# Gated linear attention on one core: two heads' outputs together, woven with the start of the output projection

## Chip, core and metric

The kernel runs on one core of a Trainium2 chip. The metric is the device time of one execution in microseconds (us), taken as the median of several runs. Lower is better.

## What is computed

The reference is a two-layer trunk over 512 positions of width 1024 in float32. The first layer mixes with a gMLP and latent attention, the second with gated linear attention; each mixer is followed by a layer norm, a squared-ReLU feed-forward network and another layer norm. The change lies in the second layer's mixer. Cut to that:

```python
def gla(q, k, v, log_a):                  # 4 heads, DK = 128, DV = 256, in chunks
    def step(state, xs):
        qi, ki, vi, gi = xs
        b = jnp.cumsum(gi, axis=2)
        o_inter = jnp.einsum('bhld,bhde->bhle', qi * jnp.exp(b), state)
        ...
        o = o_inter + jnp.einsum('bhts,bhse->bhte', attn, vi)
        b_last = b[:, :, -1:, :]
        state = (jnp.exp(b_last[:, :, 0, :])[..., None] * state
                 + jnp.einsum('bhsd,bhse->bhde', ki * jnp.exp(b_last - b), vi))
        return state, o
...
o = gla(q, k, v, log_a)
o = layer_norm(o, c_ln_g[j], c_ln_b[j]).astype(x.dtype).reshape(bn, s, hv)
y = (o * jax.nn.silu(g)) @ w_out_odd[j]
x = layer_norm(ALPHA * x + y, ln1_g[layer], ln1_b[layer])
```

## The kernel before

The kernel keeps the 512 positions as four blocks (chunks) of 128. A float32 product with a weight is made as three products of rounded halves (`mm3`, lines 159 to 161: high by high, high by low, low by high), 128x512 each, on TensorE. The halves are made by `split`: ScalarE casts the high half, VectorE subtracts to get the low half (lines 164 and 165). Weights come through three `raw` buffers by DMAs on SP's queue.

PSUM is given out in eight banks under four tags (`BANKS`, line 122): "mm" 3, "sc" 2, "o" 1, "tp" 2. A tile of a tag takes the banks of that tag in turn, so it waits until the last reader of the tile before it in that bank is done.

In `odd_mixer` each head goes through `chunk_steps` (line 1090), which makes the attention matrix `at`, the decayed query `qb`, the decayed and transposed key `kh` (transposed on TensorE, line 1161, copied by ScalarE, line 1163) and the decays `ebl`. Then `head_out` (line 1166) makes the outputs of a head, chunk by chunk: `su` = kh by V (line 1179), from which VectorE makes the next state (line 1182 for the first, line 1184 for the others), and `o1` = at by V plus qb by state (lines 1185 and 1187). Two chunks share one accumulator bank of 128x512. Each half is read by VectorE for its mean and variance (lines 1189 and 1190). After two chunks follow a reciprocal root in twelve small 128x2 steps on VectorE (`rsqrt_`, lines 173 to 182) and a thirteenth (line 1194), the normalisation of both halves on ScalarE (line 1197), and three 128x512 operations on VectorE (lines 1199, 1200, 1203), the last of which multiplies it into the gate tile `G`. `head_out` is a generator that yields after every chunk with an estimate of TensorE's time.

The heads' outputs are spread over the other work. `weave(a, b, n)` takes one step of b, then n steps of a, and so on. Head 0 is woven with the projection of head 3's query and key, head 1 with the second half of the gate's projection, head 2 with whatever is left of that (line 1266), and head 3 with `early` of `out_proj_odd` (line 1300). `early` transposes G of heads 0 and 1 (`y_T`, eight transposes a call over two banks of "tp" when two blocks are taken; line 194, then `split` into XH and XL) and runs the four first of eight row blocks of the output projection for (block, half) (0, 0), (1, 0) and (0, 1) (`part`, line 1280). Behind it stand the transposes of heads 2 and 3 and the other half of the sums, with a residual add (line 208) and its statistics (line 211).

TensorE's order is that of the program (`manual_schedule`). VectorE's order in this stage is a scheduler's, and from `in_order` (line 1305) on that of the program; ScalarE's is the scheduler's too. Each engine runs its own instructions strictly in that order.

Of the kernel before, what the change touches and what calls it, by code (L numbers as in the profile page):

```python
# [37 lines left out]
C_HEADS, C_DK, C_DV = 4, 128, 256  # L38
# [65 lines left out]
def trunk(ctx: ExitStack, tc: tile.TileContext, a: dict, out: bass.AP):  # L104
# [20 lines left out]
    def bank(name, tag=None):  # L125
        tag = tag or next(cycle)
        return ps.tile([P, 512], F32, tag=tag, name=name, bufs=BANKS[tag])
# [14 lines left out]
    def weave(a, b, n):  # L142

        live = True
        while live:
            live = False
            for g, m in ((b, 1), (a, n)):
                for _ in range(m):
                    c = next(g, None)
                    if c is None:  # L150
                        break
                    live = True
                    yield c

    def granules(w, r0, rows, kb, cols, pool=wp):
        return [granule(w[r:r + kb * P, cols], kb, cols.stop - cols.start, pool) for r in range(r0, r0 + rows, kb * P)]
# [10 lines left out]
    def rsqrt_(var, n, eps=LN_EPS):  # L167

        v = sm.tile([P, n], F32, tag=f"nv{n}", name="nv")
        w = sm.tile([P, n], F32, tag=f"nw{n}", name="nw")  # L170
        y = sm.tile([P, n], F32, tag=f"ny{n}", name="ny")
        t = sm.tile([P, n], F32, tag=f"nt{n}", name="nt")
        nc.vector.tensor_scalar(v, var, eps, None, ALU.add)
        nc.vector.tensor_scalar(w, var, eps, -0.5, ALU.add, ALU.mult)
        nc.vector.tensor_scalar(y.bitcast(I32), v.bitcast(I32), -0.5, MAGIC_RSQRT, ALU.mult, ALU.add)
        for _ in range(3):
            if n == 1:
                nc.vector.tensor_scalar(t, y, y, w, ALU.mult, ALU.mult)
            else:
                nc.vector.tensor_tensor(t, y, y, ALU.mult)  # L180
                nc.vector.tensor_tensor(t, t, w, ALU.mult)
            nc.vector.scalar_tensor_tensor(y, t, 1.5, y, ALU.add, ALU.mult)
        return y

    def tb(t):
        return slice(t * P, (t + 1) * P)

    def to_xT(src, k0, nk, t):

        for k in range(0, nk, 4):  # L190
            m = min(4, nk - k)
            pt = bank("xt", "tp")
            for j in range(m):
                nc.tensor.transpose(pt[:, j * P:(j + 1) * P], src[:, (k + j) * P:(k + j + 1) * P], ident)
            split(XH[:, k0 + k:k0 + k + m, tb(t)], XL[:, k0 + k:k0 + k + m, tb(t)],
                  pt[:, :m * P].rearrange("p (k c) -> p k c", k=m))

    def load_ln(g, b):
        nc.sync.dma_start(LG, g.partition_broadcast(P))
        nc.sync.dma_start(LB, b.partition_broadcast(P))  # L200

    def new_stats():
        return [sm.tile([P, 2, 6], F32, tag="st", name="st", bufs=8) for _ in range(NT)]
# [56 lines left out]
    def act_stat(acc, lh, ll, g, per, ks, last):  # L260

        for k in ks:
            wh, wl = g[k // per]
            mm3(acc, lh[k], ll[k], wh[:, k % per], wl[:, k % per], k == 0, k == last)

    def in_order():

        return tc.manual_schedule(engines={mybir.EngineType.DVE})

    def xblk(t):  # L270
        return [XH[:, k, tb(t)] for k in range(KD)], [XL[:, k, tb(t)] for k in range(KD)]
# [721 lines left out]
    def out_steps(gs, stats, accs):  # L993

        def mm(t, n, k0, k1):
            if (t, n) not in accs:
                accs[t, n] = bank("op"), 0
            acc, done = accs[t, n]
            act_stat(acc, *xblk(t), gs[n], 2, range(max(k0, done), k1), KD - 1)
            if k1 == KD:  # L1000
                add_half(t, n, acc, True, stats)
        return norms(mm, stats, lambda t: ff_T["now"](t))
# [13 lines left out]
    def odd_mixer(mp, v0_granules):  # L1016
# [3 lines left out]
        G = mp.tile([P, NT, HV], F32, name="G1")  # L1020
# [142 lines left out]
            nc.scalar.copy(kh[:, :NT - 1].rearrange("p c d -> p (c d)"), pt[:, :(NT - 1) * P])  # L1163
            heads[h] = (at, qb, kh, ebl)

        def head_out(h, tag="mm"):
            at, qb, kh, ebl = heads[h]
            hv = slice(h * C_DV, (h + 1) * C_DV)
            st = None
            for c2 in range(0, NT, 2):  # L1170
                op = bank("o1", tag).rearrange("p (c d) -> p c d", c=2)
                bst = sm.tile([P, 2, 6], F32, tag="bs", name="bs")
                mv = sm.tile([P, 2, 2], F32, tag="mv2", name="mv2")
                for c in (c2, c2 + 1):
                    o = op[:, c - c2]
                    sn = None
                    if c < NT - 1:
                        u = bank("su", "o")[:, :C_DV]
                        nc.tensor.matmul(u, kh[:, c], V[:, c, hv], start=True, stop=True)
                        sn = mp.tile([P, C_DV], F32, tag="state", name="state", bufs=3)  # L1180
                        if c == 0:
                            nc.vector.tensor_copy(sn, u)
                        else:
                            nc.vector.scalar_tensor_tensor(sn, st, ebl[:, c:c + 1], u, ALU.mult, ALU.add)
                    nc.tensor.matmul(o, at[:, c], V[:, c, hv], start=True, stop=c == 0)
                    if c > 0:
                        nc.tensor.matmul(o, qb[:, tb(c)], st, start=False, stop=True)
                    st = sn
                    nc.vector.bn_stats(bst[:, c - c2], o)
                    nc.vector.bn_aggr(mv[:, c - c2], bst[:, c - c2])  # L1190
                    yield 1.28 if 0 < c < NT - 1 else 0.85
                rs = rsqrt_(mv[:, :, 1], 2)
                nm = sm.tile([P, 2], F32, tag="nm", name="nm")
                nc.vector.scalar_tensor_tensor(nm, mv[:, :, 0], -1.0, rs, ALU.mult, ALU.mult)
                z = mp.tile([P, 2, C_DV], F32, tag="z", name="z", bufs=ZB)
                for i in range(2):
                    nc.scalar.activation(z[:, i], op[:, i], AF.Identity, scale=rs[:, i:i + 1], bias=nm[:, i:i + 1])
                bc = lambda w: w.unsqueeze(1).broadcast_to([P, 2, C_DV])
                nc.vector.tensor_tensor(z, z, bc(CG), ALU.mult)
                nc.vector.tensor_tensor(z, z, bc(CB), ALU.add)  # L1200
                while (True, c2 + 1, h // 2) not in done:
                    yield 0.0
                nc.vector.tensor_tensor(G[:, c2:c2 + 2, hv], G[:, c2:c2 + 2, hv], z, ALU.mult)
# [49 lines left out]
        fill.add(qk[2], 10.2)  # L1253
        fill.add(nat(G, 2 * HK + HV, 0, True), 20.5)
        ho0 = fill.add(weave(qk[3], head_out(0), 4), 14.5)
        g1w = weave(g1, head_out(1), 4)
        fill.add(g1w, 24.8)
        fill.run(2.5)
        for h in range(C_HEADS):
# [3 lines left out]
                fill.until(ho0, 1.8)  # L1263
            for _ in chunk_steps(h):
                fill.run(SLOT)
        for _ in weave(g1w, head_out(2), 3):
            pass
        return head_out, G

    def out_proj_odd(left):  # L1270
        head_out, G = left
        w = a["w_out_odd"][0]
        gs = [granules(w, 0, D, 2, slice(n * 512, (n + 1) * 512)) for n in range(2)]
        stats = new_stats()
        accs = {}

        def y_T(t, h0, nh):
            to_xT(G[:, t, h0 * C_DV:(h0 + nh) * C_DV], 2 * h0, 2 * nh, t)

        def part(t, n):  # L1280
            acc = bank("op", "mm")
            for k in range(4):
                act_stat(acc, *xblk(t), gs[n], 2, [k], KD - 1)
                yield 0.64
            accs[t, n] = acc, 4

        def early():
            y_T(0, 0, 2)
            yield 0.43
            y_T(1, 0, 2)  # L1290
            yield 0.43
            yield from part(0, 0)
            y_T(2, 0, 2)
            yield 0.43
            y_T(3, 0, 2)
            yield 0.43
            yield from part(1, 0)
            yield from part(0, 1)

        for _ in weave(early(), head_out(3, "sc"), 2):  # L1300
            pass
        load_ln(a["ln1_g"][1], a["ln1_b"][1])

        steps = out_steps(gs, stats, accs)
        with in_order():
            y_T(0, 2, 2)
            y_T(1, 2, 2)
            next(steps)
            y_T(2, 2, 2)
            y_T(3, 2, 2)  # L1310
        return steps
# [3 lines left out]
    with tc.tile_pool(name="m0", bufs=1) as mp:  # L1315
        left = even_mixer(mp)
# [5 lines left out]
    with tc.tile_pool(name="m1", bufs=1) as mp:  # L1322
        steps = out_proj_odd(odd_mixer(mp, v0))
# [41 lines left out]
```

## Time and profile before

| what | us |
|---|---|
| median of three runs | 1166.93 |
| lowest and highest of them | 1166.70 and 1167.01 |
| the profiled execution, its own time | 1167.06 |
| its span, from first to last instruction | 1165.4 |
| TensorE busy in the span | 1140.8 |
| VectorE busy | 827.6 |
| ScalarE busy | 517.0 |

The span is what the trace shows; the execution's own time is 1.66 us longer than it. A busy TensorE includes pipelined tails: the ends of matmuls are modelled, and one row's busy time lies partly under the next one's. Idle time of an engine is shown in the timeline in square brackets with what ended it.

### The profile page before, as it was taken

Reading aid. Unit: us, or ns where it says so; the run is one execution under the profiler, and the core shown is the slowest. Engines: PE = TensorE matmul, PEld = TensorE weight load, DVE = VectorE, ACT = ScalarE, POOL = GpSimd, SP = SyncE. Lnnn points to the kernel's source line nnn. Section 1 sums busy time; section 2 is a strip of 40 time slices with the busy share of each in tenths; the row PEclk is TensorE's granted clock in tenths of the full one; section 3 lists DMA queues with packets and bytes.
Section 4 is the critical chain, followed back from the end, with each engine's and each line's share of the span. In section 5 each row is a group of like instructions: output and inputs, shape, how many; then the busy total and the mean of one; then the engine's idle time right before and its main releaser. Section 6 shows DMA issues by size and latency. Waiting matters only on the chain.

```text
span 1165.4 us, 17129 instructions
## 1 busy us (share of the span) xinstructions
PE 1140.8 (98%) x6884; PEld 994.6 (85%) x6884; DVE 827.6 (71%) x1562; ACT 517.0 (44%) x801; POOL 4.5 (0%) x13
## 2 busy tenths in 40 slices
PE   8999999999999999999999999999999999999997
PEld 7988788898889998997888888778997899889986
DVE  6745687786766867658758559898767577676665
ACT  6367462444343634543264433442534436345330
POOL 0000000000000000000000000000000000000000
PEclk9999999999999999999999999999999999999999
DMA  8413143133312342224325312211133224314121
GB/s 269 125 37 109 55 130 107 37 109 109 127 62 84 128 127 84 79 79 135 75 95 145 91 55 73 73 66 62 62 125 116 90 80 142 129 38 127 55 91 55
DMA packets 84207, 111.68 MB, mean 96 GB/s; under 512 B 6080, under 2 KB 53056, under 8 KB 84128
## 3 DMA queue, kind: packets, MB, share of 16 engines
q1 hardware_dynamic: 84128, 110.59, 30.0%
q8 instruction: 54, 0.88, 0.3%
q14 instruction: 25, 0.20, 0.1%
HBM read 108.47 MB, written 2.10 MB: 95 GB/s over the span
## 4 chain that ended last, share of the span: by engine, by line
PE 89%; DVE 6%; ACT 4%; DMA 0%; issue 0%; SPq 0%; DVEq 0%; ACTq 0%
PE f L451 23%; PE f L161 10%; PE f L160 10%; PE f L159 10%; PE vg L159 3%; PE vg L160 3%; PE vg L161 3%; PE op L159 3%; PE op L161 3%; PE op L160 2%; PE sc L843 1%; PE qk L159 1%; PE qk L160 1%; PE qk L161 1%; PE o L865 1%; PE pl L1129 1%
## 5 line engine op out<-in xcount | busy, mean ns | idle before, releaser
L161 PE MATMUL f<-whi,hl 128*128 128x512 f32 x448 | 177.4, 396 | 5.5 <-DVE hl L431 5.5
L159 PE MATMUL f<-whi,hh 128*128 128x512 f32 x448 | 177.2, 396 | 1.0 <-ACT hh L430 1.0
L164 ACT CAST whi<-cr 128x1024 fp32r<-128x1024 f32 x98 | 100.8, 1048 | 174.0 <-PE f L161 81.1
L160 PE MATMUL f<-wlo,hh 128*128 128x512 f32 x448 | 176.8, 395 | 0.0
L164 ACT CAST whi<-raw 128x1024 fp32r<-128x1024 f32 (+3 forms) x117 | 118.4, 1019 | 99.1 <-PE f L451 35.7
L165 DVE TENSOR_TENSOR wlo<-raw,whi 128x1024 fp32r<-128x1024 f32 (+3 forms) x117 | 138.0, 1186 | 26.5 <-ACT whi L164 26.5
L165 DVE TENSOR_TENSOR wlo<-cr,whi 128x1024 fp32r<-128x1024 f32 x98 | 119.3, 1221 | 23.0 <-ACT whi L164 23.0
L451 PE MATMUL f<-XH,wlo 128*128 128x256 f32 x448 | 125.9, 281 | 0.0
L451 PE MATMUL f<-XH,whi 128*128 128x256 f32 x448 | 125.8, 281 | 0.0
L451 PE MATMUL f<-XL,whi 128*128 128x256 f32 x448 | 125.8, 281 | 0.0
L161 PEld LDWEIGHTS f<-whi,hl 128*128 128x128 f32 x448 | 84.3, 188 | 27.7 <-DVE hl L431 8.1
L208 DVE SCALAR_TENSOR_TENSOR XN<-XN,f 128x512 f32<-128x512 f32 (+1 forms) x113 | 74.4, 679 | 42.6 <-PE f L161 42.1
L159 PEld LDWEIGHTS f<-whi,hh 128*128 128x128 f32 x448 | 84.3, 188 | 20.8 <-ACT hh L430 1.8
L160 PEld LDWEIGHTS f<-wlo,hh 128*128 128x128 f32 x448 | 84.3, 188 | 19.3
L451 PE MATMUL f<-sl,whi 128*128 128x256 f32 x336 | 94.6, 281 | 0.0
L451 PE MATMUL f<-sh,wlo 128*128 128x256 f32 x336 | 94.5, 281 | 0.0
L451 PE MATMUL f<-sh,whi 128*128 128x256 f32 x336 | 94.5, 281 | 0.0
L431 DVE TENSOR_TENSOR hl<-r,hh 128x512 fp32r<-128x512 f32 x64 | 44.2, 690 | 60.6 <-ACT hh L430 60.6
L451 PEld LDWEIGHTS f<-XL,whi 128*128 128x128 f32 x448 | 84.4, 188 | 0.5
L451 PEld LDWEIGHTS f<-XH,whi 128*128 128x128 f32 x448 | 84.4, 188 | 0.5
L451 PEld LDWEIGHTS f<-XH,wlo 128*128 128x128 f32 x448 | 84.4, 188 | 0.0
L451 PEld LDWEIGHTS f<-sh,whi 128*128 128x128 f32 x336 | 63.3, 188 | 0.0
(268 smaller groups left out, 2396.8 us busy)
## 6 DMA issues: line engine op xcount, KB each, us to landing
raw<-in_w_ff SPq DMA_DIRECT2D x70, 512.0 KB, 4.1
cr<-in_w_ff SPq DMA_DIRECT2D x58, 512.0 KB, 4.0
raw<-in_w_in_odd SPq DMA_DIRECT2D x24, 512.0 KB, 4.2
XN<-in_x SPq DMA_DIRECT2D x16, 256.0 KB, 3.4
raw<-in_w_in_even SPq DMA_DIRECT2D x8, 512.0 KB, 4.6
raw<-in_w_out_even SPq DMA_DIRECT2D x8, 512.0 KB, 3.8
raw<-in_w_out_odd SPq DMA_DIRECT2D x8, 512.0 KB, 3.6
LB<-in_ln_b SPq DMA_DIRECT2D x4, 512.0 KB, 3.8
```

The source lines that it names most:

```text
L159: nc.tensor.matmul(acc, lh, rh, start=first, stop=False)
L160: nc.tensor.matmul(acc, lh, rl, start=False, stop=False)
L161: nc.tensor.matmul(acc, ll, rh, start=False, stop=last)
L164: nc.scalar.copy(hi, src)
L165: nc.vector.tensor_tensor(lo, src, hi.bitcast(F32), ALU.subtract)
L208: nc.vector.scalar_tensor_tensor(x, x, ALPHA if first else 1.0, acc, ALU.mult, ALU.add)
L431: late.append(lambda: nc.vector.tensor_tensor(f(hl), r, f(hh).bitcast(F32), ALU.subtract))
L451: nc.tensor.matmul(d, l, r, start=first and j == k == i == 0, stop=j == 1 and k == HK_ - 1 and i == 2, skip_group_check=True)
L843: nc.tensor.matmul(sc[:, :N], qts[t][:B_QK, h, :], KT[:, h, :N], start=True, stop=True)
L865: nc.tensor.matmul(os[t][:, h, :], pT[:, j * P:(j + 1) * P], V[:, j, h, :], start=j == 0, stop=j == t)
L1129: nc.tensor.matmul(pl[:, c * 64:(c + 1) * 64], x[:, tb(c)], x[:, tb(c)].rearrange("p (n two k) -> p n two k", two=2, k=H)[:, :, 1], start= ...
```

## The change

Head 2's outputs no longer run by themselves behind what is left of the gate's projection. Heads 2 and 3 are woven with each other, one chunk of head 3, then one of head 2, and that sequence is woven with `early`, two steps of `early` for each chunk. Both heads' accumulators come from the two "sc" banks (head 2 had "mm" before). Head 3's `su` comes from the "tp" banks, which the transposes use as well; head 2's `su` stays in the single "o" bank. The number of instructions is the same on every engine.

```diff
-        def head_out(h, tag="mm"):
+        def head_out(h, tag="mm", state_tag="o"):
             at, qb, kh, ebl = heads[h]
...
                     if c < NT - 1:
-                        u = bank("su", "o")[:, :C_DV]
+                        u = bank("su", state_tag)[:, :C_DV]
...
-        for _ in weave(g1w, head_out(2), 3):
+        for _ in g1w:
             pass
-        return head_out, G
+        return weave(head_out(2, "sc"), head_out(3, "sc", "tp"), 1), G
 
     def out_proj_odd(left):
-        head_out, G = left
+        last_heads, G = left
...
-        for _ in weave(early(), head_out(3, "sc"), 2):
+        for _ in weave(early(), last_heads, 2):
             pass
```

How instructions move is shown at three places. The first is TensorE at the third chunk of head 2. Names: `su` is the state's product, `o1` a head's accumulator, `op` the projection's, `state` the state it reads. Before:

```order
L1187 MATMUL o1_7184<-state_7189,qb_6725 128x256
L1179 MATMUL su_7229<-V1_5687,kh_6810 128x256
L1185 MATMUL o1_7226<-V1_5687,at_6511 128x256
L1187 MATMUL o1_7226<-state_7196,qb_6725 128x256
L1185 MATMUL o1_7226<-V1_5687,at_6511 128x256
L1187 MATMUL o1_7226<-state_7231,qb_6725 128x256
```

and with the change:

```order
L159 MATMUL op_7348<-whi_7185,XH_69 128x512
L160 MATMUL op_7348<-wlo_7186,XH_69 128x512
L161 MATMUL op_7348<-whi_7185,XL_70 128x512
L1179 MATMUL su_7382<-V1_5687,kh_6810 128x256
L1185 MATMUL o1_7379<-V1_5687,at_6511 128x256
L1187 MATMUL o1_7379<-state_7293,qb_6725 128x256
```

Projection products now stand ahead of head 2's third chunk; its accumulator `o1_7379` is in the bank of head 2's first one, `o1_7260`, where before `o1_7226` took another bank of three.

The second place is VectorE at the same chunk. `ny` and `nt` are the reciprocal root of head 2's first two chunks, `nm` its last step. Before, behind the state's update for `su_7229`:

```order
L165 TENSOR_TENSOR wlo_7309<-raw_7307,whi_7308 128x1024
L1190 BN_AGGR mv2_7186<-bs_7185 128x2
L1184 SCALAR_TENSOR_TENSOR state_7231<-state_7196,ebl_6729,su_7229 128x256
L173 TENSOR_SCALAR nv_7202<-mv2_7186 128x2
L174 TENSOR_SCALAR nw_7203<-mv2_7186 128x2
L1189 BN_STATS bs_7227<-o1_7226 128x6
```

and with the change:

```order
L1203 TENSOR_TENSOR G1_5688<-G1_5688,z_7331 128x2x256
L182 SCALAR_TENSOR_TENSOR ny_7357<-nt_7358,ny_7357 128x2
L1184 SCALAR_TENSOR_TENSOR state_7384<-state_7293,ebl_6729,su_7382 128x256
L180 TENSOR_TENSOR nt_7358<-ny_7357 128x2
L181 TENSOR_TENSOR nt_7358<-nt_7358,nw_7356 128x2
```

The update for the same `su` now stands in the middle of the reciprocal root; behind it come lines 180, 181 and 182 twice and line 1194, seven steps.

The third place is VectorE ahead of the last transposes of G. `z` is a normalised pair of chunks on its way into `G1`, `xt` a bank of transposes, `XN` the residual. Before:

```order
L182 SCALAR_TENSOR_TENSOR ny_7417<-nt_7418,ny_7417 128x2
L1194 SCALAR_TENSOR_TENSOR nm_7431<-mv2_7382,ny_7417 128x2
L165 TENSOR_TENSOR XL_70<-xt_7469,XH_69 128x4x128
L165 TENSOR_TENSOR XL_70<-xt_7476,XH_69 128x4x128
L1199 TENSOR_TENSOR z_7433<-z_7433,LB_73 128x512
L1200 TENSOR_TENSOR z_7433<-z_7433,LB_73 128x512
L1203 TENSOR_TENSOR G1_5688<-G1_5688,z_7433 128x2x256
L208 SCALAR_TENSOR_TENSOR XN_71<-XN_71,op_7349 128x512
```

and with the change:

```order
L165 TENSOR_TENSOR XL_70<-xt_7476,XH_69 128x4x128
L1203 TENSOR_TENSOR G1_5688<-G1_5688,z_7435 128x2x256
L181 TENSOR_TENSOR nt_7444<-nt_7444,nw_7442 128x2
L182 SCALAR_TENSOR_TENSOR ny_7443<-nt_7444,ny_7443 128x2
L1194 SCALAR_TENSOR_TENSOR nm_7457<-mv2_7381,ny_7443 128x2
L208 SCALAR_TENSOR_TENSOR XN_71<-XN_71,op_7270 128x512
L211 BN_STATS st_7232<-XN_71 128x6
L1199 TENSOR_TENSOR z_7459<-z_7459,LB_73 128x512
L1200 TENSOR_TENSOR z_7459<-z_7459,LB_73 128x512
L1203 TENSOR_TENSOR G1_5688<-G1_5688,z_7459 128x2x256
```

Two pairs of chunks, head 3's `z_7435` and head 2's `z_7459`, now pass here where one did, the three operations of the last pair stand behind the first residual add, and five 128x512 operations, from line 1199 of `z_7435` to its line 1203, stand among the last steps of head 2's reciprocal root.

## Rows read from the trace of the kernel before

**Rows 1.** Page, busy us of TensorE, share of the span, instructions (then other engines).

```profile
PE 1140.8 (98%) x6884; PEld 994.6 (85%) x6884; DVE 827.6 (71%) x1562; ACT 517.0 (44%) x801; POOL 4.5 (0%) x13
```

**Rows 2.** Windows: length, busy of PE, PEld, DVE, ACT, POOL; clock; DMA.

```profile
747.00:754.00 7.00, 5.49 (x24) 3.90 (x23) 6.83 (x23) 1.53 (x2) 0.00 (x0) 1.00 0.73 216
762.00:773.00 11.00, 10.76 (x53) 8.35 (x52) 10.46 (x33) 4.64 (x10) 0.00 (x0) 1.00 0.01 1
```

**Rows 3.** Timeline, TensorE, head 2's outputs: start, busy, instruction, [idle before <- releaser].

```profile
747.03 0.60 PE L1179 MATMUL su<-V,kh 128*128 128x256 f32 x2
747.46 0.59 PE L1185 MATMUL o<-V,at 128*128 128x256 f32 x2
748.37 0.70 PE L1179 MATMUL su<-V,kh 128*128 128x256 f32 x2 [0.32 <-DVE state L1182]
...
750.29 0.70 PE L1179 MATMUL su<-V,kh 128*128 128x256 f32 x2 [0.35 <-DVE state L1184]
...
752.69 0.70 PE L1185 MATMUL o<-V,at 128*128 128x256 f32 x2 [0.84 <-DVE bs L1189]
```

**Rows 4.** Timeline, TensorE, the weave and the transposes behind it.

```profile
760.31 0.39 PE L160 MATMUL op<-wlo,XH 128*128 128x512 f32 x1
760.54 0.40 PE L161 MATMUL op<-whi,XL 128*128 128x512 f32 x1
761.08 0.70 PE L1185 MATMUL o<-V,at 128*128 128x256 f32 x2
761.62 0.59 PE L1187 MATMUL o<-state,qb 128*128 128x256 f32 x2
...
768.52 1.07 PE L194 MATMUL xt<-ident,G 128*128 128x128 f32 x8
769.83 0.50 PE L159 MATMUL op<-whi,XH 128*128 128x512 f32 x1 [0.24 <-ACT XH L164]
...
770.56 0.50 PE L161 MATMUL op<-whi,XL 128*128 128x512 f32 x1
...
773.00 1.29 PE L194 MATMUL xt<-ident,G 128*128 128x128 f32 x8
```

**Rows 5.** Timeline, VectorE, the same stretch.

```profile
747.88 0.44 DVE L1182 COPY state<-su 128x256 f32<-128x256 f32 x1
...
748.57 1.20 DVE L165 TENSOR_TENSOR wlo<-raw,whi 128x1024 fp32r<-128x1024 f32 x1
749.69 0.17 DVE L1190 BATCH_NORM_AGGREGATE mv<-bs 128x2 f32<-128x6 f32 x1
...
759.88 0.46 DVE L1184 SCALAR_TENSOR_TENSOR state<-state,ebl,su 128x256 f32<-128x256 f32 x1
...
768.58 0.15 DVE L180 TENSOR_TENSOR nt<-ny 128x2 f32<-128x2 f32 x1
768.77 0.16 DVE L181 TENSOR_TENSOR nt<-nt,nw 128x2 f32<-128x2 f32 x1
...
771.22 0.69 DVE L1199 TENSOR_TENSOR z<-z,LB 128x512 f32<-128x512 f32 x1
...
772.67 0.69 DVE L1203 TENSOR_TENSOR G<-G,z 128x512 f32<-128x512 f32 x1
```

**Rows 6.** Timeline, ScalarE, the same stretch.

```profile
747.23 0.48 ACT L1163 COPY kh<-kh 128x384 f32<-128x384 f32 x1 [0.51 <-PE kh L1161]
748.81 1.05 ACT L164 CAST whi<-raw 128x1024 fp32r<-128x1024 f32 x1 [1.10 <-DMA raw<-in_w_out_odd]
...
761.53 1.02 ACT L1197 ACTIVATE z<-o,nm,ny 128x256 f32<-128x256 f32 x2 [4.38 <-DVE nm L1194]
...
769.20 1.07 ACT L164 CAST XH<-xt 128x512 fp32r<-128x512 f32 x2 [2.71 <-PE xt L194]
```

**Rows 7.** Windows at the end of the span, columns as in rows 2.

```profile
1156.00:1158.00 2.00, 1.41 (x12) 1.21 (x11) 0.52 (x2) 0.00 (x0) 0.00 (x0) 1.00 0.00 0
1161.00:1162.00 1.00, 0.00 (x0) 0.00 (x0) 1.00 (x2) 0.00 (x0) 0.00 (x0) 0.77 0.00 0
```

## The prediction, made before the changed kernel ran

> **What bounds the kernel now.** Read first the page's busy shares: TensorE is busy for 98% of the span [rows 1], so whatever does not shorten a wait of TensorE is worth nothing, and whatever adds one is paid in full. Then the windows: the 7 us in which head 2's outputs run alone hold only 5.49 us of TensorE work, against 10.76 of 11 us in the weave behind [rows 2]. Then TensorE's own timeline. A pair of 128x256 products is shown busy for 0.59 to 0.60 us, yet the next pair starts 0.43 us later: 0.16 us of a row's busy time is a tail under the next one. A pair that starts behind a wait takes 0.70, which is 0.11 more [rows 3]. So a wait shown as w costs w + 0.16 + 0.11 on this engine. Head 2 alone pays three: 0.32 for the copied state, 0.35 for the next state, 0.84 for the statistics that must read an accumulator before its other half is written: 0.59 + 0.62 + 1.11 = 2.3 us. In the weave and behind it [rows 4] the product at 761.08 is 0.31 late (the one before starts at 760.54 and streams for 0.23), the first projection product behind the transposes at 769.83 is 0.43 late with another 0.16 for its low half, and the transposes at 773.00 lose about 0.26 to the gate; with restarts 1.5 us. **All of TensorE's waits here add up to 3.8 us**, the most that any reordering can win. The clock is 1.00 throughout [rows 2].
>
> **The change, part by part.** TensorE has the same instructions in both; only order and banks change, SP and POOL keep their queues row by row (the layer-norm load on SP waits for the last reader of the old constants, and that reader, like the load's own first reader, moves with TensorE). So the cost is new waits less the 3.8 us of old ones. I followed the new order on the three engines by hand from the last common place, the transposes of kh, with durations from the rows and a hand-over of 0.04 to 0.05 us between engines (the state copied at 747.88 ends at 748.32, TensorE goes on at 748.37) [rows 3, 5]. Followed in this way the old order gives 3.7 us of waits where the trace has 3.8.
>
> 1. Head 3 now goes first, and its kh is the one just transposed. ScalarE's copy ends at 747.71 [rows 6], where head 2's had long been there: the first su starts at 747.75 instead of 747.03, **0.72**.
> 2. Head 3's su now takes turns in the two banks of the transposes, so the second group of transposes waits for VectorE's copy of the state. On VectorE a weight split (1.12 to the next start, row 748.57 to the one behind) now stands ahead of that copy: 747.88 + 1.12 + 0.44 = 749.44, TensorE was ready at 749.16: **0.3** [rows 5].
> 3. The next split needs the last weight tile, whose cast on ScalarE runs from 748.81 (its DMA) to 749.86 [rows 6]. Queued behind it on VectorE is the low half of the first transposed block, ready at 751.8, for which the third projection product waits from 751.4: **0.5**.
> 4. The third su of head 3 takes the bank of the transposes issued just ahead of it. Cover is gone: the first block of them must pass ScalarE's cast (half of 1.07 and its tail, 0.6) and VectorE's subtraction (0.7, as other 128x512 operations there) before su may write [rows 5, 6]. With tail, hand-overs and 0.24 in which VectorE is still at small steps that is 1.7, of which the second block's transposes cover 0.44: **1.3**.
> 5. Head 2 now shares the two "sc" banks with head 3, where it had three "mm" banks. Its third product must wait until ScalarE has read its first accumulator, and that waits for its reciprocal root. On VectorE the state update that needs the su just ahead on TensorE (0.46; next start 0.36 later) stands in front of seven dependent small steps, 0.19 to 0.20 apart [rows 5]. From the su: tail 0.16, hand-over 0.04, state 0.36, six spacings 1.20, last step 0.16, hand-over 0.04, normalisation on ScalarE 1.02 [rows 6], hand-over 0.04: **3.0**. Queued behind the waiting product are all projection steps left in the weave. From below, steps that found the state ready early would pay 1.4 less; from above nothing is longer on that chain. I take 3.0: order and rows agree.
> 6. The transposes behind the weave: ScalarE normalises head 3's second half ahead of the casts: 0.6 in place of 0.43, and 0.4 in place of 0.16 for the low half.
> 7. The last transposes need G with both heads multiplied in. Before, head 3's last product ended at 761.62 + 0.59 = 762.2, 10.8 us of TensorE's time ahead of them (773.00) [rows 4], and even so they lost 0.26: the chain is 11.1 long at its old, unhurried pace. Now head 2's last product ends one projection pair, eight transposes (0.9), item 6 and four blocks of products ahead of them: 1.4 + 0.9 + 1.2 + 2.8 = 6.3 us of issue, 6.1 from the product's shown end. The chain: statistics 1.0, eleven dependent spacings and the last step 2.4, with five vector operations of 0.60 among them (3.0, less 0.4 where they fill a spacing), normalisation 1.06, a residual add and its statistics that now stand ahead (0.6 more), then three dependent operations 0.73 apart (771.22 to 772.67 is two spacings; 2.2 with the last) [rows 5]: 9.9 us. **3.7** late, unrounded. From below, with none of the five operations between, 1.2; from above, the old pace of 11.1, 5.0. I take 3.7, since the order has all five there.
>
> Sum of the new waits: 0.72 + 0.3 + 0.5 + 1.3 + 3.0 + 0.6 + 0.4 + 3.7 = 10.5, and eight restarts at 0.11, 0.9: 11.4 us. Less 3.8 is **7.7 us slower** (11.5 less 3.8 with unrounded starts). The profiled execution took 1167.06 us (span 1165.4 and 1.7 around it), so it becomes 1174.8; the median of the runs shown is 0.13 below it, 1166.93, so I say **1174.7**. Behind the last transposes the projection goes on without a wait in both orders, and no later stage has slack to take 7.7 us back.
>
> **The rivals.**
> *The weave covers the waits.* Head 2's three waits (2.3 us) vanish under projection products, and the new ones are as short as those of head 3 in the old weave (0.31 and a restart): 1166.9 - 2.3 = 1164.6. For it: two projection blocks, 1.4 us, stand between each two steps of a head [rows 4], longer than any of the three waits shown. Against it: 1.4 us covers a state update, but not the reciprocal root and normalisation of item 5, nor item 7. It decides below a sum of new waits of 3.8 us; items 1 to 4 alone with restarts are 3.3. 3 in 100. The Trainium skill, Perfetto Trace Analysis, section Optimization Strategy, says that interleaving regimes with different limits may improve performance; by that rule it would come out as here, and the window of head 2, with idle TensorE beside busy VectorE, is such a regime, but VectorE at 10.46 of 11 us in the weave [rows 2] says that the other regime is the same one.
> *Gains and new waits meet.* Items 5 and 7 both come out at their lower ends, 1.6 and 1.2: 1174.7 - 1.4 - 2.5 = 1170.8; to be within 0.2% items 1 to 4 would have to shrink by half as well (1.6 less). 5 in 100 for within 0.2% (2.3 us, about what a measurement of this kernel can tell from no change).
> *Only one of the two long waits comes.* If VectorE has finished head 2's chain in time for the last transposes (item 7 at 1.2): 1172.2; if item 5 pays 1.6: 1173.3. 12 in 100.
> *The clock falls in a long wait.* After the last matmul (1.41 us into 1156 to 1158, so 1157.4) the granted clock stays 1.00 until 0.54 us into the window 1161 to 1162, whose mean is 0.77 (half rate, 1.2 GHz, for the rest) [rows 7]: it had been idle for 4.1 us by then. My longest wait, 3.7, is shorter, but not by much. Had the clock fallen and stayed low for as long again, matmuls would lose half of 4.1, an estimate: 2.0 us, 1176.7. 10 in 100. The Trainium skill, TensorE: Matmul & The Clock Gate, section HAM oscillation, warns that long pauses between bursts of matmuls drop the clock to half rate and that the next burst then starts slow; no row here shows how long it stays there.
>
> **How the numbers follow.** The forecast itself has 70 in 100. Slower: 70 + 12 + 10 = 92; within 0.2%: 5; faster: 3. The forecast's own range is 1173.5 to 1176.0 (item 7 from 2.5 to its upper end 5.0). To hold 8 in 10 I reach up past the clock case, 1177.0, and down to where one long wait is partly covered, 1172.5.
>
> **What would show it.** In the changed profile: an idle of TensorE of about 2.9 us on L1185 released by ScalarE's z (item 5), one of about 3.5 us on L194 released by G on L1203 (item 7), about 1.1 us on L1179 released by VectorE's XL (item 4), and 0.7 us on L1179 released by the kh copy. The state waits on L1179 and the one on bs at L1185 are gone. It is wrong if L1185 waits for z under 1 us, or if TensorE reaches the last transposes with G already multiplied; then the span is below 1171. A clock under 1.00 between 765 and 790 would be the fourth rival.

## The result, and the profile after

| what | before | after |
|---|---|---|
| median of the runs on this chip, us | 1166.93 | 1177.77 |
| lowest and highest, us | 1166.70 and 1168.45 | 1176.25 and 1179.18 |
| the profiled execution, us | 1167.06 | 1178.16 |
| mean granted clock of that execution | 0.998 | 0.995 |

The ratio is 1.009, with a 95% interval from 1.0079 to 1.0101: slower, as forecast, but 3.1 us above the predicted 1174.7 and 0.8 us above the upper end of the range. Both kernels repeat with steps of about 1.6 us between their executions, to which the last experiment comes back.

TensorE's waits between 740 and 800 us in the kernel after, the waits view (releaser, then total us, times, longest):

```profile
PE xt L194 <- DVE G L1203: 3.6, 1, 3.6
PE o L1185 <- ACT z L1197: 2.9, 1, 2.9
PE su L1179 <- DVE XL L165: 1.2, 1, 1.2
PE op L161 <- DVE XL L165: 1.0, 2, 0.7
PE su L1179 <- ACT kh L1163: 0.6, 1, 0.6
PE op L159 <- ACT XH L164: 0.4, 1, 0.4
PE xt L194 <- DVE state L1182: 0.2, 1, 0.2
```

These are the prediction's items, by releaser and by instruction, and nothing else: G is item 7, z is item 5, XL at su is item 4, XL at op items 3 and 6, kh is item 1, XH item 6, state item 2. The state waits on L1179 and the one on bs at L1185 [rows 3] are gone. TensorE's timeline has them in their places (start, busy, instruction, idle before and releaser):

```profile
747.56 0.70 PE L1179 MATMUL su<-V,kh 128*128 128x256 f32 x2 [0.57 <-ACT kh L1163]
...
749.30 0.66 PE L194 MATMUL xt<-ident,G 128*128 128x128 f32 x4 [0.18 <-DVE state L1182]
...
751.97 0.50 PE L161 MATMUL op<-whi,XL 128*128 128x512 f32 x1 [0.68 <-DVE XL L165]
...
759.20 0.70 PE L1179 MATMUL su<-V,kh 128*128 128x256 f32 x2 [1.17 <-DVE XL L165]
...
765.51 1.22 PE L1185 MATMUL o<-V,at 128*128 128x256 f32 x2 [2.87 <-ACT z L1197]
766.52 1.06 PE L1187 MATMUL o<-state,qb 128*128 128x256 f32 x2
...
767.81 0.63 PE L160 MATMUL op<-wlo,XH 128*128 128x512 f32 x1
768.24 0.63 PE L161 MATMUL op<-whi,XL 128*128 128x512 f32 x1
...
769.02 0.39 PE L160 MATMUL op<-wlo,XH 128*128 128x512 f32 x1
...
775.42 0.50 PE L159 MATMUL op<-whi,XH 128*128 128x512 f32 x1 [0.37 <-ACT XH L164]
...
776.44 0.50 PE L161 MATMUL op<-whi,XL 128*128 128x512 f32 x1 [0.29 <-DVE XL L165]
...
782.68 1.94 PE L194 MATMUL xt<-ident,G 128*128 128x128 f32 x8 [3.65 <-DVE G L1203]
784.27 0.78 PE L159 MATMUL op<-whi,XH 128*128 128x512 f32 x1
```

Look at the busy column as well. A pair that starts behind a wait is shown with 0.70 at 747.56 and 759.20, but with 1.22 at 765.51; a 128x512 product is shown with 0.39 at 769.02, but with 0.63 at 767.81, and its follower starts 0.43 us later instead of 0.23. The same work runs at about half speed behind the two long waits. The windows say why (length, busy of PE, PEld, DVE, ACT, POOL, then the granted clock):

```profile
762.50:765.50 3.00, 0.14 (x1) 0.00 (x0) 1.70 (x11) 1.02 (x2) 0.00 (x0) 1.00 0.00 0
765.50:769.00 3.50, 3.49 (x8) 2.83 (x9) 2.49 (x5) 0.00 (x0) 0.00 (x0) 0.51 0.00 0
769.00:773.00 4.00, 4.00 (x19) 3.37 (x18) 2.12 (x12) 0.00 (x0) 0.00 (x0) 1.00 0.00 0
...
779.00:782.50 3.50, 0.03 (x1) 0.00 (x0) 3.33 (x5) 0.83 (x2) 0.00 (x0) 1.00 0.00 0
782.50:786.00 3.50, 3.32 (x12) 3.06 (x13) 1.42 (x3) 1.93 (x3) 0.00 (x0) 0.51 0.44 162
786.00:790.00 4.00, 4.00 (x18) 3.21 (x18) 1.76 (x4) 3.22 (x5) 0.00 (x0) 1.00 0.76 232
```

In this execution the clock still reads 1.00 while TensorE is idle. It falls to 0.5, that is 1.2 GHz, as the matmuls start again, and is back at 2.4 GHz some 3.4 us later. Half of 3.4 us at each of two places is 1.7 us each, 3.4 us together, and 7.7 + 3.4 = 11.1 is what the two profiled executions differ by (1178.16 less 1167.06). That is the theory to be tested.

### The profile page after: what moved, and what is told of

The parts are those of the page before. It is cut to its first block, busy times and chain, and to the rows that moved or that the text cites. A ratio compares the mean times of both kernels' runs of the same rounds, so it can differ in the third digit from the quotient of the medians.

```text
span 1176.4 us, 17131 instructions
## 1 busy us (share of the span) xinstructions
PE 1144.3 (97%) x6884; PEld 997.2 (85%) x6884; DVE 829.9 (71%) x1562; ACT 517.0 (44%) x801; POOL 4.8 (0%) x13
## 4 chain that ended last, share of the span: by engine, by line
PE 88%; DVE 7%; ACT 4%; DMA 1%; issue 1%; SPq 0%; DVEq 0%; ACTq 0%
PE f L451 23%; PE f L161 10%; PE f L160 10%; PE f L159 10%; PE vg L159 3%; PE op L161 2%; PE vg L160 2%; PE vg L161 2%; PE op L159 2%; PE op L160 2%; PE sc L843 1%; PE qk L159 1%; PE qk L160 1%; PE qk L161 1%; PE o L865 1%; PE pl L1129 1%
## 5 line engine op out<-in xcount | busy, mean ns | idle before, releaser
L161 PE MATMUL f<-whi,hl 128*128 128x512 f32 x448 | 177.4, 396 | 5.5 <-DVE hl L431 5.5
L161 PEld LDWEIGHTS f<-whi,hl 128*128 128x128 f32 x448 | 84.2, 188 | 27.8 <-DVE hl L431 8.1
L451 PEld LDWEIGHTS f<-sl,whi 128*128 128x128 f32 x336 | 63.3, 188 | 0.0
```

The lines of the kernel that those rows point to most:

```text
L161: nc.tensor.matmul(acc, ll, rh, start=False, stop=last)
L451: nc.tensor.matmul(d, l, r, start=first and j == k == i == 0, stop=j == 1 and k == HK_ - 1 and i == 2, skip_group_check=True)
```

## The experiments

**Theory A**: the waits cost the 7.7 us of the prediction, and the clock falls behind each of the two long ones, for 1.7 us apiece. **Theory B**: the clock is incidental, and the waits and their knock-on alone cost what was measured. Each run stands beside runs of the kernel before on the same chip.

### Fed waits: matmuls without use in the two long waits

Products of the identity by itself are issued into free banks where TensorE waits for z and for G: 24 and 32 of them in the first run, 12 and 16 in a second. The edit, written out more plainly than in the kernel that ran:

```diff
+        feed = lambda acc, n: [nc.tensor.matmul(acc[:, :P], ident, ident, start=True, stop=True) for _ in range(n)]
...
+                    if (h, c) == (2, 2): feed(bank("op", "mm"), 24)        # second run: 12
                     nc.tensor.matmul(o, at[:, c], V[:, c, hv], start=True, stop=c == 0)
...
             next(steps)
+            feed(bank("warm", "sc"), 32)                                    # second run: 16
```

(The "op" bank then serves the projection block that would have taken it.)

> The changed kernel, with small matmuls of the identity (128x128) put on TensorE inside its two long waits: 24 behind head 2's third su (2.6 us of a wait of 3.0), 32 ahead of the last transposes (3.5 of 3.8). Nobody reads their results; the waits end when they did. Theory A, the 3.1 us beyond the forecast are TensorE at half rate behind the two long waits (granted clock 0.50 for about 3.4 us each, 1.7 lost each): granted clock back to 0.998, time 1177.8 - 3.4 = 1174.4, which is the forecast without the clock. Theory B, the clock rows are incidental and the waits alone cost 11: no less than 1177.5.

Measured: 1181.86 us (1180.34 to 1183.25), 1.0117 of the kernel before, interval 1.0104 to 1.0131. The experiment was mis-sized. Each of these float32 products is two instructions, so they take twice what I had reckoned, 5.5 and 7.3 us, and outlast the waits (TensorE's timeline):

```profile
762.47 5.52 PE L1087 MATMUL op<-ident 128*128 128x128 f32 x48
...
779.49 7.31 PE L1087 MATMUL warm<-ident 128*128 128x128 f32 x64
```

The granted clock was 1.00 through the stretch, which speaks for A, but as more work than the waits could hold was added, the time decides nothing, though it lies on the side that had been set for B (no less than 1177.5). Hence the second run with half of it.

> The kernel after, with the dummy products of the first run cut to 12 in front of head 2's third product (24 instructions of 0.11 us, 2.6 us) and 16 in front of the last transposes (32, 3.5 us), so that they fit into the two waits of 2.9 and 3.65 us instead of outlasting them. Theory A (waits cost 7.7 us, two falls of the clock 1.7 each): the granted clock stays 1.00 from 740 to 800, TensorE ends its dummies before z and G come, the products behind them start where they do in the kernel after (765.5 and 782.7, within 0.4), and the time is before + 7.7 us, 1.0066, from 7.2 to 8.4. Theory B (the clock is incidental, the waits alone cost what was measured): before + 11 us, 1.0095, with or without dummies.

Measured: 1175.67 us (1174.48 to 1180.14, 6 runs), 1.0073 of the kernel before (1168.02), interval 1.006 to 1.0086; the kernel after itself, run beside it (below), 1177.73. The timeline, and two windows:

```profile
762.42 2.84 PE L1087 MATMUL op<-ident 128*128 128x128 f32 x24
765.46 0.70 PE L1185 MATMUL o<-V,at 128*128 128x256 f32 x2 [0.20 <-ACT z L1197]
...
777.22 3.73 PE L1087 MATMUL warm<-ident 128*128 128x128 f32 x32
781.02 1.07 PE L194 MATMUL xt<-ident,G 128*128 128x128 f32 x8
```

```profile
766.00:770.00 4.00, 4.00 (x19) 3.35 (x18) 2.86 (x11) 0.00 (x0) 0.00 (x0) 1.00 0.02 4
...
782.00:786.00 4.00, 4.00 (x19) 3.22 (x19) 2.32 (x4) 3.61 (x5) 0.00 (x0) 1.00 0.73 219
```

This is the cleanest test. Head 2's third product starts at 765.46, where it starts in the kernel after (765.51): z comes no sooner. But its pair takes 0.70, not 1.22, and the last transposes start at 781.02 instead of 782.68. Those 1.66 us are the first fall's price. Work was added and the kernel became faster: by 2.1 us in the median, though the six runs and the four beside them overlap. The profiled execution took 1174.96, which is 7.9 above that of before and 3.2 below that of after (8.0 above the middle of the kernel before's faster executions on this chip, 1167.0, and 2.8 below the execution of the kernel after profiled on it): the waits alone, without a fall, cost what the prediction's sum said. (The highest of the six runs, 1180.14 at a mean clock of 0.994, was not profiled.) Theory B falls.

### The kernel after once more

> The kernel after itself, timed on the chip on which the other three of this call run, so that they stand against it and not only against the kernel before. Theory A: before + 11.1 us less what the kernel before itself loses in executions in which its own clock falls once; the granted clock at half rate in two stretches of 3 to 4 us, behind the waits for z and for G. Theory B: before + 11 us, and the stretches at half rate need not be there.

Measured: 1177.73 us (1176.19 to 1179.83, 4 runs), 1.0087, interval 1.0074 to 1.01. The same seven waits to 0.1 us, and the same two stretches at half rate. In the nine executions of this kernel on two chips the mean clock and the time go together: 1176.19 and 1176.25 us at 0.997, 1177.69 to 1178.16 at 0.995, 1179.18 at 0.994 (one, 1179.83, at 0.995 stands apart). So a fall is likely behind each long wait, but not certain.

### Pauses put into the kernel before

To see the clock without the change, the last chain of G in the kernel before gets two or four more dependent operations on VectorE, a multiplication by one each, so that its last transposes wait longer. Written out more plainly than in the kernel that ran:

```diff
                 nc.vector.tensor_tensor(z, z, bc(CB), ALU.add)
+                for _ in range(2 if (h, c2) == (3, 2) else 0):              # other run: 4
+                    nc.vector.tensor_scalar(z, z, 1.0, None, ALU.mult)
```

> The kernel before, with two more 128x512 operations on VectorE (z times 1.0) ahead of the last multiplication into G: TensorE's wait ahead of the last transposes grows by two dependent spacings of 0.73, from 0.26 to about 1.7 to 2.5 us (a scheduler places them). Theory A, a wait costs its length and the clock falls only behind about 3 us of idle or more: 1166.9 + 1.5 to 2.4 = 1168.4 to 1169.3, clock 0.998. Theory B, any pause costs more than itself: above 1170.

> The kernel before with four such operations: the wait ahead of the last transposes becomes about 3.2 to 4.0 us. Theory A: its length, 2.9 to 3.9, and one fall of the clock, 1.7: 1171.5 to 1172.5, with one stretch of about 3.4 us at granted clock 0.50 behind the wait. Theory B (the clock does not matter): 1169.8 to 1170.8. The difference to the run with two operations is 1.5 by B and 3.2 by A.

Measured: 1170.39 us (1168.74 to 1172.12, 11 runs), ratio 1.0021 from 1.0012 to 1.003; and 1172.97 us (1170.26 to 1174.23, 5 runs), ratio 1.0039 from 1.0027 to 1.0052. The two pauses in the timeline, each with windows behind it, first the one with two operations:

```profile
776.99 1.25 PE L194 MATMUL xt<-ident,G 128*128 128x128 f32 x6 [2.09 <-DVE G L1203]
...
774.00:778.00 4.00, 1.91 (x12) 1.48 (x10) 2.80 (x6) 0.54 (x1) 0.00 (x0) 0.92 0.42 131
778.00:782.00 4.00, 4.00 (x14) 3.19 (x13) 1.38 (x2) 3.47 (x5) 0.00 (x0) 0.66 0.61 180
```

and the one with four:

```profile
776.92 1.54 PE L194 MATMUL xt<-ident,G 128*128 128x128 f32 x6 [3.02 <-DVE G L1203]
...
773.90:775.90 2.00, 0.01 (x1) 0.00 (x0) 1.97 (x5) 0.00 (x0) 0.00 (x0) 1.00 0.76 240
775.90:776.90 1.00, 0.00 (x0) 0.00 (x0) 0.94 (x2) 0.00 (x0) 0.00 (x0) 0.50 0.11 45
776.90:782.70 5.80, 5.78 (x17) 4.81 (x18) 1.38 (x2) 4.00 (x5) 0.00 (x0) 0.50 0.49 156
```

The clock fell behind a shown idle of 2.09 us in one and of 3.02 us in the other, both shorter than the 3.7 that the prediction had taken to be short enough. In the second it fell 1 us before the matmuls came back and stayed at 1.2 GHz for 6.8 us, 5.8 of them with work. Half of that, 2.9 us, is what this one fall cost, more than the 1.7 reckoned.

So the forecast for the first of these runs, that so short a wait would not take the clock, was wrong. With two operations, five of the eleven runs lie at 1168.7 to 1169.2 (mean clock 0.998 or 0.999), within the 1168.4 to 1169.3 of a wait without a fall. The other six lie at 1170.4 to 1172.1 (0.997 to 0.995), above the 1170 that had been set for "any pause costs more than itself". The profiled one, 1172.12, has a second fall, at 336 us, which the edit does not touch. With four operations the median is 0.5 above the 1171.5 to 1172.5 forecast, and the two medians differ by 2.6, between the 1.5 of B and the 3.2 of A; so here the windows decide, and not the medians.

The fall isn't certain here either: the run of 1170.26 with four operations has a mean clock of 0.998, as the kernel before has, and is 3.4 us slower than the middle of that kernel's faster executions on this chip (1166.9 of 1166.48 to 1167.49; the others lie from 1168.31 to 1169.32), which is about the pause alone; the other four, at 0.994 to 0.996, took 1172.8 to 1174.2.

### One step of the projection for each chunk

```diff
-        for _ in weave(early(), last_heads, 2):
+        for _ in weave(early(), last_heads, 1):
```

The heads then end sooner, and more of the projection stands between them and the last transposes. The rival here (C) is that the two heads' chains fill VectorE, so that the last transposes are late whatever TensorE has ahead of them.

> The changed kernel with one step of the projection per chunk instead of two, so that half of the projection products are left for behind the heads' last chunk. Theory A, item 7's wait comes from the weave having used up the products that covered head 2's last chain: that wait goes (from 3.65 to under 0.5), the other waits become shorter or longer by less than 1 us each (su behind the transposes about 1.4, o behind z about 2.6), and no wait is long enough for the clock: waits come to 6.5 where the kernel before has 3.7, so 1166.9 + 2.8 = 1169.7. Rival C, the cost is the two heads' chains on VectorE that have to be done at the same time, and the end waits for them whatever stands there: above 1174.

Measured: 1171.42 us (1169.61 to 1172.92, 10 runs), ratio 1.0025 from 1.0016 to 1.0034. The wait for z and the last transposes, which now have none:

```profile
758.93 1.21 PE L1185 MATMUL o<-V,at 128*128 128x256 f32 x2 [2.43 <-ACT z L1197]
...
777.65 1.04 PE L194 MATMUL xt<-ident,G 128*128 128x128 f32 x8
```

C falls: item 7 was a matter of what stands ahead on TensorE. The forecast of 1169.7 took no wait here to be long enough for the clock, and that was wrong: it fell behind the wait for z alone (0.62 from 758 to 762, in the profiled execution of 1171.30). Four runs without a lower mean clock (0.998 or 0.999) took 1169.6 to 1170.2.

### Head 2's accumulator in a bank of its own

```diff
-                op = bank("o1", tag).rearrange("p (c d) -> p c d", c=2)
+                op = bank("o1", tag.split()[c2 // 2 % len(tag.split())]).rearrange("p (c d) -> p c d", c=2)
...
-        return weave(head_out(2, "sc"), head_out(3, "sc", "tp"), 1), G
+        return weave(head_out(2, "sc o", "tp"), head_out(3, "sc", "tp"), 1), G
```

> The kernel after, with head 2's second accumulator in the banks of the third projection block's kind instead of in a bank shared with head 3, and both heads' states in the transposes' banks. The prediction's item 5 says that head 2's third product waits 3.0 us because it takes the accumulator that ScalarE has yet to read. With the bank changed, followed by hand in the same way: that wait is gone, two waits for the low half of about 1.8 and 1.3 us stand at the states, 2.7 us are left at the last transposes, 8.6 us in all against 3.7 before: before + 4.9 us without a fall of the clock, + 6.6 with one behind the last wait. If item 5 were something else than the bank (the chain of head 2 late in any case, theory C), the wait would stand at another product of head 2 or at the last transposes with the same 3 us, and the time would be that of the kernel after.

(The text speaks of banks of the third projection block's kind; as the diff shows, the second accumulator has the single "o" bank, and head 2's states, which had it, have "tp". So two things of head 2 change here.)

Measured: 1174.16 us (1173.24 to 1175.41, 5 runs), ratio 1.0058 from 1.0045 to 1.0071. Two rows of TensorE's timeline, and a window behind the second:

```profile
751.82 0.70 PE L1179 MATMUL su<-V,kh 128*128 128x256 f32 x2 [1.74 <-DVE XL L165]
...
778.02 1.11 PE L194 MATMUL xt<-ident,G 128*128 128x128 f32 x8 [2.66 <-DVE G L1203]
```

```profile
778.00:782.00 4.00, 3.98 (x16) 3.33 (x17) 1.77 (x3) 3.32 (x5) 0.00 (x0) 0.61 0.70 221
```

No product of head 2 waits for z any more, so item 5 was the bank. The waits at the states and at the last transposes stand about as walked (1.74, 1.18 and 2.66 shown; 1.8, 1.3 and 2.7 expected). The profiled execution, 1173.24, is 6.2 above the middle of the kernel before's faster executions there, 1167.0; less 4.9 for the waits this leaves 1.3 for the one fall that the window shows. The window itself says 1.7: a mean of 0.61 over 4 us is 3.1 us at half rate, and the next 2 us, at 0.92, hold another 0.3. The walked 4.9 would then be some 0.4 too long.

### One more projection block ahead of the last transposes

```diff
             next(steps)
+            next(steps)
             y_T(2, 2, 2)
```

> The kernel after, with one more block of projection products issued ahead of the last transposes. Item 7 says that these are late by the chain on VectorE behind head 2's last product, against a fixed amount of TensorE's work ahead of them. With 1.4 us or more of work moved ahead of them the wait falls from 3.65 to about 1.5 us, and the sum of the waits to 9.3 us against 3.7 before: before + 5.6 us, and by theory A one fall of the clock (1.7) behind the wait for z but none behind the short one: before + 7.3 us, 1.0063. Theory B: before + 11 less 2.1 = before + 8.9 us.

Measured: 1174.33 us (1173.98 to 1175.83, 5 runs), ratio 1.006 from 1.0048 to 1.0072. The last transposes, and two windows of this run:

```profile
784.92 1.06 PE L194 MATMUL xt<-ident,G 128*128 128x128 f32 x8 [1.47 <-DVE G L1203]
```

```profile
336.00:340.00 4.00, 3.56 (x9) 2.86 (x10) 1.69 (x3) 1.84 (x3) 0.00 (x0) 0.61 0.00 0
...
768.00:772.00 4.00, 4.00 (x15) 3.25 (x14) 1.81 (x4) 0.00 (x0) 0.00 (x0) 0.71 0.00 0
```

The wait is 1.47 as walked, and behind it the transposes run at full rate (1.06, not 1.94). Three runs lie at 1174.0 to 1174.3, which is 7.0 to 7.3 above 1167.0, as A has it; B's 8.9 are not there. The other two, one of them the profiled one, took 1175.8, which is 8.8 above and would fit B. In the profiled one the first window tells where the 1.6 us more come from: the clock also fell at 336 us, in the feed-forward of the first layer, which the change does not touch. The other one has the same mean clock, 0.995, but no trace.

### Head 3's states back in their own bank

```diff
-        return weave(head_out(2, "sc"), head_out(3, "sc", "tp"), 1), G
+        return weave(head_out(2, "sc"), head_out(3, "sc"), 1), G
```

> The kernel after, with one argument left out: head 3's state products go back to the bank of their own, and no longer take turns in the transposes' banks. Item 4 says that the 1.2 us wait at the third state product is for that bank (the low half of the transposes issued just ahead of it), and item 2 the same of the second transposes. Theory A: both waits are gone; followed by hand the same way, head 3's second pair of products then waits for ScalarE's z of its own first pair by 1.3 us instead, the other waits stay where they are (0.7 for the low half, 3.0 for z of head 2, 3.7 for G), so the sum is that of the kernel after within 0.4 us and so is the time: 1.0087, from 1.007 to 1.010. Rival D (the low half is late in any case because VectorE's queue is full, the bank only shows it): the 1.2 us stay at the state product or at the next user of that low half, and the time is that of the kernel after too, but with the releaser XL unchanged.

Measured: 1177.89 us (1177.49 to 1177.91, 4 runs), ratio 1.009 from 1.0075 to 1.0105. The waits for XL at su and for the state are gone, and in their place (TensorE's timeline):

```profile
759.66 0.70 PE L1185 MATMUL o<-V,at 128*128 128x256 f32 x2 [1.22 <-ACT z L1197]
```

Items 2 and 4 were the bank, as A has it, and D falls; a wait taken away here comes back at the next step of the same chain.

### A faster kernel: the low halves last

The fall at 336 stands behind a wait of TensorE that the kernel before has as well, here in that kernel's timeline:

```profile
334.24 0.50 PE L159 MATMUL f<-whi,hh 128*128 128x512 f32 x1 [0.28 <-ACT hh L430]
334.58 0.40 PE L160 MATMUL f<-wlo,hh 128*128 128x512 f32 x1
336.19 0.51 PE L161 MATMUL f<-whi,hl 128*128 128x512 f32 x1 [1.21 <-DVE hl L431]
```

This is the kernel before with another order of products at that place, and nothing of the change:

```diff
-            for k in range(4):
+            for k, part in [(k, p) for p in "hl" for k in (2, 3, 0, 1)] if t == n == 0 else [(k, "hl") for k in range(4)]:
                 hh, hl = hq[c][i, k // 2]
                 wh, wl = got_w["w2", c, n, k // 2]
-                mm3(acc, hh[:, k % 2, tc_], hl[:, k % 2, tc_], wh[:, k % 2], wl[:, k % 2], k == 0, k == 3)
+                ...
```

where part "h" issues the two products with the high half of the hidden block and "l" the one with its low half.

> The kernel before, and none of the change: in the feed-forward, where the first output block of a chunk starts, the products of the high halves of all four hidden blocks are issued ahead of those of the low halves. In the kernel before, TensorE waits there four times for the low half of the block made last (1.2 us each, at 292, 336, 880 and 924, with 0.2 to 0.3 for its high half), and two of the profiled runs above show the clock at half rate from 336 to 340 behind that wait, where the kernel before as profiled shows 1.00. Theory A (short idles take the clock too, in some executions): the waits give 1.5 to 1.9 us each where the order fills them, 6 to 7.7 us in all, and the two groups of the kernel before's times (about 1166.8 and 1168.3) become one group: 1159 to 1161 us, 0.992 to 0.994 of the kernel before on this chip. Theory B (clock incidental): the two groups stay 1.5 us apart. Should VectorE, not TensorE, set the pace there, the products behind wait instead and only 0 to 3 us are gained.

Measured: 1159.20 us (1158.95 to 1159.73, 5 runs) against 1167.0 (9 runs), ratio 0.9931 from 0.9919 to 0.9944. The same place in its timeline:

```profile
333.20 0.39 PE L513 MATMUL f<-wlo,hh 128*128 128x512 f32 x1
333.44 1.24 PE L515 MATMUL f<-whi,hl 128*128 128x512 f32 x4
334.51 0.39 PE L512 MATMUL f<-whi,hh 128*128 128x512 f32 x1
```

No wait is left there, and the total for hl on L161 goes from 5.5 us in six places to 0.6 in two. The nine runs of the kernel before beside it fall into five from 1166.33 to 1167.00 and four from 1168.21 to 1168.38, 1.6 us apart; the five of this kernel lie within 0.8 us. This fits theory A, by which the second group goes with the short idles, but five runs do not prove it: the four of the run before this one, which has all the waits, lie within 0.4 us too. That the upper runs of the kernel before lost their 1.6 us at 336, and not at one of the three like places, isn't shown, since none of them was profiled; runs of two other kernels were, and both show it there. This version beats both kernels of the case.

## Why the prediction was wrong in size

Its sum of waits was right within half a microsecond. Adding to each idle shown the 0.16 us tail of the prediction:

| item | forecast | measured |
|---|---|---|
| 1, kh copy | 0.72 | 0.57 + 0.16 = 0.73 |
| 2, state copy | 0.3 | 0.18 + 0.16 = 0.34 |
| 3, first low half | 0.5 | 0.68 + 0.16 = 0.84 |
| 4, su in the transposes' bank | 1.3 | 1.17 + 0.16 = 1.33 |
| 5, accumulator's bank | 3.0 | 2.87 + 0.16 = 3.03 |
| 6, behind the transposes | 0.6 + 0.4 | 0.53 + 0.45 |
| 7, last transposes | 3.7 | 3.65 + 0.16 = 3.81 |

Only item 3 is off by clearly more than 0.1. The measured ones are 11.1; with eight restarts (0.9) and less the old waits (3.8) this is 8.2, where the run with fed waits shows 7.9 and the prediction had 7.7. (Put on the median of 1166.93, its 7.7 gives 1174.6; the 1174.7 carries a rounding.) With 3.4 for two falls the 8.2 makes 11.6, half a microsecond more than the 11.1 by which the profiled executions differ; that rest is open. Banks and chains are as argued: items 2, 4, 5 and 7 were each moved or taken away by one edit, and moved by what the same walk through the order gave.

**The step that failed** is the rival "the clock falls in a long wait", which had 10 in 100 and one fall. The prediction took from rows 7 that the clock had stayed at 1.00 for 4.1 us of idle at the end of the span, and concluded that 3.7 us of wait was short of it. That was one sighting, of one idle, in one execution; it told when the clock fell there, not how much idle the clock stands. The same idle at the end of the span differs between the traces: the clock stays up for 4.9 us of it in the run with four operations, for 3.2 in the kernel after and for 2.2 in the run with the low halves last (the first and the last of these in windows from the last product on; the clock is the third number from the right).

```profile
1163.50:1168.40 4.90, 0.00 (x0) 0.00 (x0) 4.51 (x11) 0.29 (x1) 0.00 (x0) 1.00 0.00 0
1168.50:1169.50 1.00, 0.00 (x0) 0.00 (x0) 0.00 (x0) 0.00 (x0) 0.00 (x0) 0.50 1.03 385
...
1149.30:1151.40 2.10, 0.00 (x1) 0.00 (x0) 1.96 (x6) 0.29 (x1) 0.00 (x0) 1.00 0.00 0
1151.60:1152.60 1.00, 0.00 (x0) 0.00 (x0) 0.93 (x4) 0.00 (x0) 0.00 (x0) 0.50 0.00 0
```

In the waits, the profiled executions showed a fall behind 3.65, 3.02, 2.87, 2.66, 2.43 and 2.09 us of shown idle, every time, and none behind 1.74 or 1.47. Behind 0.28 and 1.21 us with two products between them, at 336, two of them had one. And as the rival was priced for one wait, the second fall was missing from it too: its price per fall, 2.0, was near the 1.7 that half of 3.4 us makes. The two falls that the 1174.7 lacked, 3.2 to 3.4 us in all, are not waits but slower work behind waits.

The Trainium skill, TensorE: Matmul & The Clock Gate, section HAM oscillation, had said that pauses between bursts of matmuls bring the clock to half rate and that the next burst starts slow. The trace agrees, twice in this kernel: idle at 1.00, then 0.51 from the first matmul on. The prediction quoted it and let its own row outweigh it, though that row didn't contradict it.

The rival that the weave covers the waits (1164.6) fell as argued, since VectorE and ScalarE, not TensorE's work, set the pace of the heads. "Only one of the two long waits comes" did not happen either, but the run with one step of the projection for each chunk is that case made by hand: no wait at the last transposes, 1171.4 us.

## What to carry to other kernels

On an engine that is 98% busy, a reordering is worth at most the waits that it can remove, so count these first (3.8 us in the stretch changed here) and then follow the new order by hand through banks and dependent chains: this gave every wait in its place. A wait of TensorE is then not only its own length: price a possible fall of the clock behind each long one, and behind short ones where several lie close together, and widen the range by that price rather than argue it away from one quiet stretch. Where a product waits for a low half, work with the high halves that is already there may be put in between.

## What was not expected of the hardware

- In the two long waits of the kernel after as first profiled, the granted clock reads 1.00 through the idle and falls as the matmuls come back: 0.51 in the next 3.5 us, 1.00 again behind that. In other executions it fell earlier, 1 us before the matmuls in the run with four operations. (At the end of the span it falls in the idle itself [rows 7].) A fall with 3.4 us at half rate cost up to 1.7 us, the one with 6.8 us cost 2.9, and behind the same wait it comes in some executions and, by their mean clock, not in others.
- Steps of some 1.6 us between executions of one kernel, which look like noise, go with the mean clock, which is lower by about 0.0015 with each (0.998, 0.997, 0.995, 0.994). Where an execution above the lowest group was profiled (1171.30, 1172.12 and 1175.78 us in three of the runs), its trace has the falls to show for it; for the kernel before none was profiled.
- Work added to a wait made a kernel faster, by 2.1 us in the median (1177.73 to 1175.67, four and six runs).
- A float32 128x128 product by the identity is two instructions of 0.11 us; a transpose by the same identity is one.
